# Column-wise Newton rounds, lookups by halving additions, and a new pace for the gathered expert rows in a two-layer diffusion backbone

## The chip, the cores and the metric

The kernel runs on one core of a Trainium2 chip. The metric is the device time of one execution in microseconds (us); a kernel's time is the median of its runs. Engines are named as the profile names them: PE (TensorE matmul), PEld (its weight loads), DVE (VectorE), ACT (ScalarE), POOL (GpSimd), SP (SyncE, whose queue issues most DMAs).

## The reference

Two layers over 256 latent tokens and 256 context tokens of width 1024, all in float32. The part that matters here is what surrounds the norms and the expert layer:

```python
def _rmsnorm(x, g):
    y = xf * lax.rsqrt(jnp.mean(xf * xf, axis=-1, keepdims=True) + EPS)
    return (y * g).astype(x.dtype)

# per layer: h = modulate(rmsnorm(x)); three token mixers; x += gate * mix
#            h2 = modulate(rmsnorm(x)); x += gate * _peer(h2)

def _peer(h, w_pq, peer_keys, peer_down, peer_up):        # 8 heads, 128 x 128 = 16384 experts
    s = einsum("blhpd,hpkd->blhpk", q, peer_keys)
    sv, si = lax.top_k(s, 16)                             # two sets of 16 per head
    cand = sv[..., 0, :, None] + sv[..., 1, None, :]
    cidx = si[..., 0, :, None] * 128 + si[..., 1, None, :]
    top_s, pos = lax.top_k(cand, 16)
    eidx = take_along_axis(cidx, pos)                     # the lookup
    gate = softmax(top_s)
    a = einsum("tkd,td->tk", peer_down[eidx], h)
    return einsum("tk,tkd->td", gate * gelu(a), peer_up[eidx])
```

## The kernel before

Activations lie transposed, 128 of the 1024 features in the partitions and tokens in the free dimension. Every weight is loaded by SP in pieces of 128x512 (`wpart`, L75 to L83), split by ACT into a high part (`wh`, L81) and by DVE into the remainder (`wl`, L82), and used in three matmuls (`mm3`, L91 to L93, or L789 to L791 for the up projection). So each matmul group waits for an SP load, an ACT copy and a DVE subtraction, and anything that stands ahead of that subtraction on DVE, which works in order, holds up PE.

**Norms.** `rstd` sums squares with matmuls against ones (L221), forms the mean (L225), and `newton` (L232 to L238) takes the inverse square root: a first guess (L234) and three rounds of three DVE instructions, each on the result of the one before. Its 128x2 operands hold one column for each block of 128 tokens. Then two scaled identities (L229), a broadcast by matmul (L245), four multiplications (L271), the modulation (L283) and the split (L285, L286) follow, and only then can the next matmuls (L91) start.

**Routing.** `topk` finds 16 of 112 candidates per head and then looks up the two key indices of each: a one-hot tile of 4 heads x 16 x 16 in bf16 is made (L607), multiplied with the indices (L612) and summed over one axis (L614), once for each of two index sets and two groups of four heads. It runs six times (24 sums in all): two times for the context tokens of layer 0, woven into the attention, and four times in `routes`.

**Experts of layer 0.** 128 of the context tokens take their 128 experts each by gathering (`rows`): 256 units, each an indirect DMA of 128 rows of 4 KB issued by POOL (L693) into one of three `gx` buffers, and one DVE pass over 128x1024: a dot product with `hot` for a down row (L706), or a weighted accumulation for an up row (L713). A gather is issued two units ahead, so its buffer comes free when the unit before the current one has been worked. The other 384 tokens go densely through all 128 blocks of 128 experts (`experts`, a step for each block): 18 matmuls of 512 columns, and for blocks from 60 on also the down projection with 24 matmuls of 384 columns. For the first 60 blocks that projection was done earlier and its result lies in DRAM (`E0`); SP loads it (`ge<-E`, L743), and DVE multiplies it with the gates (L752) and splits it (L754, L755). Steps are worked four blocks ahead.

`experts_both` calls the generator of units at a pace: `ROWS_S` units a step while the block ahead is still one of the 60, `ROWS_N` afterwards. Here "the first part" is the steps with loaded blocks and "the second part" those with a down projection. What is left of the units is drained after the last step (`drain(rows)`, L913), before the norm of layer 1. The instruction order of each engine comes from a scheduler that works from this program order.

Of the kernel before, what the change touches and what calls it, by code (L numbers as in the profile page):

```python
# [16 lines left out]
OP = mybir.AluOpType  # L17
AX = mybir.AxisListType
# [8 lines left out]
WINDOWS = (2, 4, 8, 16)  # L27
TG = 16
EARLY0, EARLY1 = 60, 88
ROWS_O, ROWS_A, ROWS_S, ROWS_N = 1, 0.5, 0.4, 2.6  # L30
SC0, SC1, R0, R1 = 0.5, 0.5, (0.36, 0.46, 0.34), (0.53, 0.9, 0.66)
FILL = (0, 3, 6)
PARTS = ((1, 3), (2, 5), (4,))
# [6 lines left out]
class Net:  # L40
# [191 lines left out]
    def newton(self, v, r, t):  # L232
        nc = self.nc
        nc.vector.tensor_scalar(r.bitcast(I32), v.bitcast(I32), -0.5, float(0x5F3759DF), op0=OP.mult, op1=OP.add)  # L234
        for _ in range(3):
            nc.vector.scalar_tensor_tensor(t, r, -0.5, r, op0=OP.mult, op1=OP.mult)
            nc.vector.tensor_mul(t, t, v)
            nc.vector.scalar_tensor_tensor(r, t, 1.5, r, op0=OP.add, op1=OP.mult)  # L238

    def bcast(self, dg):  # L240

# [319 lines left out]
    def topk(self, sv, si, out):  # L561
        nc, kp = self.nc, self.k
        ts = kp.tile([128, 8, 16], F32, name="tsc", bufs=1)
        pos = kp.tile([128, 128], U32, name="pos", bufs=1)


        for h4 in range(2):
            cd = self.f2([128, 4, 112])
            ra, rb = sv[:, 8 * h4:8 * h4 + 8:2, :], sv[:, 8 * h4 + 1:8 * h4 + 8:2, :]
            nc.vector.tensor_tensor(cd[:, :, 0:64].rearrange("p h (a b) -> p h a b", a=4),  # L570
                                    ra[:, :, 0:4].unsqueeze(3).to_broadcast([128, 4, 4, 16]),
                                    rb.unsqueeze(2).to_broadcast([128, 4, 4, 16]), op=OP.add)
            nc.vector.tensor_tensor(cd[:, :, 64:112].rearrange("p h (a b) -> p h a b", a=12),
                                    ra[:, :, 4:16].unsqueeze(3).to_broadcast([128, 4, 12, 4]),
                                    rb[:, :, 0:4].unsqueeze(2).to_broadcast([128, 4, 12, 4]), op=OP.add)
            for i in range(4):
                hd = 4 * h4 + i
                scr = self.f1([128, 112])
                yield from self.top16(ts[:, hd, :], pos[:, hd * 16:(hd + 1) * 16], cd[:, i, :], scr)
                yield  # L580

        sb = kp.tile([128, 2, 128, 2], BF, name="sb", bufs=1)
        for d in range(2):
            nc.vector.tensor_copy(sb.rearrange("p w (h a) d -> p w h a d", h=8)[:, :, :, :, d],
                                  si.rearrange("p (h w) a -> p w h a", w=2))
        g = kp.tile([128, 8, 16], F32, name="gate", bufs=1)
        sm = kp.tile([128, 8, 2], F32, name="gsum", bufs=1)
        nc.vector.tensor_sub(g, ts, ts[:, :, 0:1].to_broadcast([128, 8, 16]))
        nc.scalar.activation(g, g, AF.Exp)
        nc.vector.reduce_sum(sm[:, :, 0], g, axis=AX.X)  # L590
        nc.vector.reciprocal(sm[:, :, 1], sm[:, :, 0])
        nc.vector.tensor_mul(g, g, sm[:, :, 1:2].to_broadcast([128, 8, 16]))
        pu = self.f2([128, 4, 128], U32)
        nc.vector.tensor_scalar(pu[:, 0, :], pos, 4, None, op0=OP.logical_shift_right)
        nc.vector.tensor_scalar(pu[:, 1, :], pos, 2, None, op0=OP.logical_shift_right)
        nc.vector.tensor_scalar(pu[:, 2, :], pos, 15, None, op0=OP.bitwise_and)
        nc.vector.tensor_scalar(pu[:, 3, :], pos, 3, None, op0=OP.bitwise_and)
        pb = kp.tile([128, 2, 128], BF, name="pb", bufs=1)
        nc.vector.scalar_tensor_tensor(pb[:, 0, :], pu[:, 1, :], -12.0, pu[:, 0, :], op0=OP.add, op1=OP.max)
        nc.vector.scalar_tensor_tensor(pb[:, 1, :], pu[:, 0, :], 4.0, pu[:, 2, :], op0=OP.is_lt, op1=OP.mult)  # L600
        nc.vector.tensor_tensor(pb[:, 1, :], pb[:, 1, :], pu[:, 3, :], op=OP.max)
        ij = kp.tile([128, 2, 128], F32, name="ij", bufs=1)
        for w in range(2):
            for h4 in range(2):
                ks = slice(64 * h4, 64 * h4 + 64)
                oh = self.f2([128, 4, 16, 16], BF)
                nc.vector.tensor_tensor(  # L607
                    oh, self.iota16.unsqueeze(1).to_broadcast([128, 4, 16, 16]),
                    pb[:, w, ks].rearrange("p (h k) -> p h k", h=4).unsqueeze(2).to_broadcast([128, 4, 16, 16]),
                    op=OP.is_equal)  # L610
                o4 = oh.rearrange("p h a (k d) -> p (h a) k d", d=2)
                nc.vector.tensor_tensor(o4, o4, sb[:, w, ks, :].unsqueeze(2).to_broadcast([128, 64, 8, 2]), op=OP.mult)  # L612
                yield
                nc.vector.reduce_sum(ij[:, w, ks].rearrange("p (h k) -> p h k", h=4),  # L614
                                     oh.rearrange("p h a k -> p h k a"), axis=AX.X)
                yield
        out += [ij, g]

# [490 lines left out]
```

## Time and profile before

| | |
|---|---|
| median of 3 runs | 3106.73 us (3104.7 to 3107.01) |
| the profiled execution's own time | 3093.76 us |
| its span | 3092.0 us |
| PE, PEld busy | 2896.5 us (94%), 2597.3 us (84%) |
| DVE busy | 2341.6 us (76%) |
| ACT, POOL busy | 1443.6 us (47%), 322.3 us (10%) |
| DMA | 708.36 MB, mean 229 GB/s |

The span runs from the first to the last instruction of the profiled execution. That execution took 13 us less than the median of the runs shown; durations are read from it, and the median is what a prediction has to meet. PE is the busiest engine, but its share is a mean over stages, and matmuls overlap, so a busy PE is not one at its peak.

### The profile page before, as it was taken

To read this page: it belongs to the slowest core of one execution; us is meant where nothing else is said; L and a number is where in the kernel's file an instruction comes from. 1 tells how busy PE (TensorE), PEld (TensorE's weight loads), DVE (VectorE), ACT (ScalarE), POOL (GpSimd) and SP (SyncE) were. 2 spreads that over 40 slices of the span, in tenths; PEclk is the share of its full clock that TensorE was granted. 3 is DMA by queue.
4 is the path that set the end of the run, shared out by engine and by line. 5 is a ranking of instruction groups with operands and counts; after the bars stand their busy time and mean duration, and the time that the engine had idled before them with its cause. 6 is when DMAs were issued, how large, how long until landed. Compare 5 with 4: busy or idle time off the path is not lost.

```text
span 3092.0 us, 53067 instructions
## 1 busy us (share of the span) xinstructions
PE 2896.5 (94%) x18335; PEld 2597.3 (84%) x18335; DVE 2341.6 (76%) x5278; ACT 1443.6 (47%) x2820; POOL 322.3 (10%) x260
## 2 busy tenths in 40 slices
PE   7999899798999999999999996699999999999998
PEld 5799878798999777799998995589889998788997
DVE  6677779889988566688787887755799886676666
ACT  5565444443444333344433332354545555555554
POOL 0000000121000011134333344000000000000000
PEclk8999999999999999999999997799999999999999
DMA  7574443676666877799898987543657778888664
GB/s 249 171 233 144 139 129 116 213 249 199 199 221 213 289 251 263 248 309 327 314 320 308 319 294 264 177 152 123 186 159 228 242 235 283 296 267 286 203 201 141
DMA packets 413519, 708.36 MB, mean 229 GB/s; under 512 B 38336, under 2 KB 160960, under 8 KB 409152
## 3 DMA queue, kind: packets, MB, share of 16 engines
q1 hardware_dynamic: 376384, 570.73, 56.4%
q0 software_dynamic: 36864, 134.23, 13.2%
q8 instruction: 143, 2.34, 0.3%
q14 instruction: 128, 1.05, 0.1%
HBM read 638.49 MB, written 66.32 MB: 228 GB/s over the span
## 4 chain that ended last, share of the span: by engine, by line
PE 43%; DMA 10%; DVE 7%; issue 3%; POOL 1%; ACT 1%; DVEq 0%; SPq 0%; ACTq 0%; POOLq 0%
PE acc L790 6%; PE mm L91 6%; PE acc L791 6%; PE mm L92 6%; PE acc L789 6%; PE mm L93 6%; DMA gx<-in_up,eidx 3%; DMA ge<-E 3%; DVE wl L82 2%; DMA raw<-in_up 1%; DMA gx<-in_down,eidx 1%; PE acc L662 1%; PE acc L91 1%; PE acc L92 1%; PE acc L93 1%
## 5 line engine op out<-in xcount | busy, mean ns | idle before, releaser
L81 ACT CAST wh<-raw 128x512 fp32r<-128x512 f32 x1604 | 973.7, 618 | 834.1 <-PE mm L93 196.3
L82 DVE TENSOR_TENSOR wl<-raw,wh 128x512 fp32r<-128x512 f32 x1604 | 1079.8, 689 | 278.7 <-ACT wh L81 269.3
L91 PE MATMUL mm<-hH,wh 128*128 128x256 f32 (+1 forms) x2432 | 755.6, 311 | 12.8 <-ACT ge L731 8.0
L92 PE MATMUL mm<-hH,wl 128*128 128x256 f32 (+1 forms) x2432 | 748.9, 308 | 12.5 <-DVE wl L82 12.5
L93 PE MATMUL mm<-hL,wh 128*128 128x256 f32 (+1 forms) x2432 | 746.2, 307 | 0.0
L790 PE MATMUL acc<-wl,f 128*128 128x512 f32 x1280 | 506.6, 396 | 16.8 <-DVE wl L82 15.7
L789 PE MATMUL acc<-wh,f 128*128 128x512 f32 x1280 | 502.9, 393 | 5.0 <-ACT f L754 5.0
L791 PE MATMUL acc<-wh,f 128*128 128x512 f32 x1280 | 502.3, 392 | 0.0
L92 PEld LDWEIGHTS mm<-hH,wl 128*128 128x128 f32 x2432 | 467.2, 192 | 19.5 <-DVE wl L82 15.0
L91 PEld LDWEIGHTS mm<-hH,wh 128*128 128x128 f32 x2432 | 466.8, 192 | 18.9 <-ACT ge L731 9.1
L93 PEld LDWEIGHTS mm<-hL,wh 128*128 128x128 f32 x2432 | 466.2, 192 | 0.1
L790 PEld LDWEIGHTS acc<-wl,f 128*128 128x128 f32 x1280 | 242.1, 189 | 77.4 <-DVE wl L82 30.4
L693 POOL DMA_INDIRECT gx<-in_down,eidx x128 | 169.7, 1326 | 1295.5 <-DVE f L713 566.0
L789 PEld LDWEIGHTS acc<-wh,f 128*128 128x128 f32 x1280 | 242.3, 189 | 53.4 <-ACT f L754 5.3
L791 PEld LDWEIGHTS acc<-wh,f 128*128 128x128 f32 x1280 | 242.0, 189 | 49.9
L752 DVE TENSOR_TENSOR ge<-ge,f 128x256 f32<-128x256 f32 (+1 forms) x384 | 136.5, 380 | 180.5 <-DMA ge<-E 147.9
L754 ACT CAST f<-ge 128x384 fp32r<-128x384 f32 (+1 forms) x256 | 117.1, 459 | 284.3 <-DVE ge L752 278.2
L731 ACT ACTIVATE ge<-mm 128x384 f32<-128x384 f32 (+1 forms) x256 | 112.0, 438 | 222.2 <-PE mm L93 215.3
L91 PE MATMUL acc<-hH,wh 128*128 128x256 f32 x688 | 210.2, 306 | 2.0 <-ACT hH L285 2.0
L713 DVE SCALAR_TENSOR_TENSOR f<-gx,av,f 128x1024 f32<-128x1024 f32 x128 | 164.0, 1282 | 56.8 <-DMA gx<-in_up,eidx 56.4
L706 DVE CUSTOM_DVE_ANT_0 gx<-gx,f 128x1024 f32<-128x1024 f32 x128 | 156.3, 1221 | 60.4 <-DMA gx<-in_down,eidx 60.2
L92 PE MATMUL acc<-hH,wl 128*128 128x256 f32 x688 | 199.2, 290 | 0.9 <-DVE wl L82 0.9
(221 smaller groups left out, 3840.8 us busy)
## 6 DMA issues: line engine op xcount, KB each, us to landing
raw<-in_downT SPq DMA_DIRECT2D x512, 256.0 KB, 4.0
raw<-in_up SPq DMA_DIRECT2D x512, 256.0 KB, 4.3
raw<-in_wmod SPq DMA_DIRECT2D x192, 256.0 KB, 3.8
raw<-in_winc SPq DMA_DIRECT2D x172, 256.0 KB, 3.1
G<-f SPq DMA_DIRECT2D x40, 1024.0 KB, 6.0
f<-G SPq DMA_DIRECT2D x32, 1024.0 KB, 7.2
raw<-in_wpq SPq DMA_DIRECT2D x96, 256.0 KB, 3.4
raw<-in_wo SPq DMA_DIRECT2D x48, 256.0 KB, 2.6
```

The costliest lines, as they stand in the source:

```text
L81: nc.scalar.copy(H, r)
L82: self.last = nc.vector.tensor_sub(L, r, H.bitcast(F32)).ins
L91: t.matmul(out, lhsT=wH, rhs=xH, start=first, stop=False)
L92: t.matmul(out, lhsT=wL, rhs=xH, start=False, stop=False)
L93: t.matmul(out, lhsT=wH, rhs=xL, start=False, stop=last)
L693: nc.gpsimd.indirect_dma_start(out=r, out_offset=None, in_=self.h["up"][0] if up else self.h["down0"], in_offset=bass.IndirectOffsetOnAxis ...
L706: nc.vector.tensor_tensor_reduce(r, r, hot[:, 0, :], op0=OP.mult, op1=OP.add, scale=1.0, scalar=0.0, accum_out=av[:, k:k + 1])
L713: nc.vector.scalar_tensor_tensor(hot[:, 1, :], r, av[:, k:k + 1], hot[:, 1, :], op0=OP.mult, op1=OP.add)
L752: nc.vector.tensor_mul(y, y, Gg[:, :, c, :])
L789: m(p[t][half], lhsT=aH[:, a], rhs=H[:, 0], start=(i == 0), stop=False)
L790: m(p[t][half], lhsT=aH[:, a], rhs=L[:, 0], start=False, stop=False)
L791: m(p[t][half], lhsT=aL[:, a], rhs=H[:, 0], start=False, stop=(i == 127))
```

## The change

Three things change: `newton` works each column by itself with two dependent instructions a round (the factor of -0.5 is put into `v` once); the sum of each lookup becomes three additions of halves in place and a fourth that writes the result; and the pace of the gathered units becomes 0.75 and 2.75 a step, from 0.4 and 2.6.

```diff
-ROWS_O, ROWS_A, ROWS_S, ROWS_N = 1, 0.5, 0.4, 2.6
+ROWS_O, ROWS_A, ROWS_S, ROWS_N = 1, 0.5, 0.75, 2.75
...
     def newton(self, v, r, t):
         nc = self.nc
         nc.vector.tensor_scalar(r.bitcast(I32), v.bitcast(I32), -0.5, float(0x5F3759DF), op0=OP.mult, op1=OP.add)
+        nc.vector.tensor_scalar(v, v, -0.5, None, op0=OP.mult)
+
+        cs = [slice(i, i + 1) for i in range(v.shape[1])]
         for _ in range(3):
-            nc.vector.scalar_tensor_tensor(t, r, -0.5, r, op0=OP.mult, op1=OP.mult)
-            nc.vector.tensor_mul(t, t, v)
-            nc.vector.scalar_tensor_tensor(r, t, 1.5, r, op0=OP.add, op1=OP.mult)
+            for c in cs:
+                nc.vector.scalar_tensor_tensor(t[:, c], r[:, c], r[:, c], v[:, c], op0=OP.mult, op1=OP.mult)
+            for c in cs:
+                nc.vector.scalar_tensor_tensor(r[:, c], t[:, c], 1.5, r[:, c], op0=OP.add, op1=OP.mult)
...
-                nc.vector.reduce_sum(ij[:, w, ks].rearrange("p (h k) -> p h k", h=4),
-                                     oh.rearrange("p h a k -> p h k a"), axis=AX.X)
+
+                for n in (8, 4, 2):
+                    nc.vector.tensor_tensor(oh[:, :, 0:n], oh[:, :, 0:n], oh[:, :, n:2 * n], op=OP.add)
+                nc.vector.tensor_tensor(ij[:, w, ks].rearrange("p (h k) -> p h k", h=4), oh[:, :, 0], oh[:, :, 1],
+                                        op=OP.add)
```

In the changed kernel lines after `newton` stand 4 further on, and those after the lookup 7. The first place is DVE at the end of the layer-0 expert steps and into the norm that follows, in the kernel before. L820 (24 instructions) adds the experts' result to `xT`, L225 opens the norm, L706 and L713 are the two kinds of gathered unit.

```order
2605 L706 ISA gx,av<-gx,f_3782 128x1024
2606 L706 ISA av 128x1
2607 L175 MEMSET f_21222 128x512
2608 L820 SCALAR_TENSOR_TENSOR xT<-acc,mods_93,xT 128x128 x24
2609 L713 SCALAR_TENSOR_TENSOR f_3782<-gx,av,f_3782 128x1024
2610 L706 ISA gx,av<-gx,f_3782 128x1024
2611 L706 ISA av 128x1
2612 L713 SCALAR_TENSOR_TENSOR f_3782<-gx,av,f_3782 128x1024
```

The same place in the changed kernel, from the last gathered unit (L720 is what L713 was, L827 what L820 was, L762 what L755 was).

```order
2670 L720 SCALAR_TENSOR_TENSOR f_3810<-gx,av,f_3810 128x1024
2671 L759 TENSOR_TENSOR ge<-ge,f_20464 128x256
2672 L759 TENSOR_TENSOR ge<-ge,f_20466 128x128
2673 L82 TENSOR_TENSOR wl<-raw,wh 128x512
2674 L762 TENSOR_TENSOR f_21096<-ge,f_21095 128x384
2675 L82 TENSOR_TENSOR wl<-raw,wh 128x512 x6
2676 L175 MEMSET f_21302 128x512
2677 L827 SCALAR_TENSOR_TENSOR xT<-acc,mods_93,xT 128x128 x24
2678 L176 CAST f_21302<-sc_87 128x16x4
```

No gathered unit stands behind the `xT` updates any more: before, 235 of the 256 stood ahead of the first of them and 21 behind, now all 256 stand ahead. Counted by the splits of the blocks on DVE (L755), the fourth block's split had 23 units ahead of it and the 56th 43; now it is 24 and 62.

The second place is the norm ahead of layer 1's routing on DVE, before. L82 is a weight's subtraction, L236 to L238 one Newton round; two rounds of three are shown.

```order
2983 L236 SCALAR_TENSOR_TENSOR rs<-rs 128x2
2984 L82 TENSOR_TENSOR wl<-raw,wh 128x512
2985 L237 TENSOR_TENSOR rs<-rs 128x2
2986 L82 TENSOR_TENSOR wl<-raw,wh 128x512
2987 L238 SCALAR_TENSOR_TENSOR rs<-rs 128x2
2988 L236 SCALAR_TENSOR_TENSOR rs<-rs 128x2
2989 L237 TENSOR_TENSOR rs<-rs 128x2
2990 L82 TENSOR_TENSOR wl<-raw,wh 128x512
2991 L238 SCALAR_TENSOR_TENSOR rs<-rs 128x2
```

The same two rounds in the changed kernel (L240 is the first step of a round, L242 the second, each once for a column).

```order
3018 L240 SCALAR_TENSOR_TENSOR rs<-rs 128x1 x2
3019 L242 SCALAR_TENSOR_TENSOR rs<-rs 128x1
3020 L82 TENSOR_TENSOR wl<-raw,wh 128x512
3021 L242 SCALAR_TENSOR_TENSOR rs<-rs 128x1
3022 L240 SCALAR_TENSOR_TENSOR rs<-rs 128x1 x2
3023 L242 SCALAR_TENSOR_TENSOR rs<-rs 128x1
3024 L82 TENSOR_TENSOR wl<-raw,wh 128x512
```

Between L225 and L229 of this norm 9 subtractions stood before, and 6 stand now. On PE, ACT and SP few instructions moved (165 of 19617 on PE), and POOL's order is the same.

## Rows read from the trace of the kernel before

**Rows 1.** Windows: stretch, its length, busy us (and instructions) of PE, PEld, DVE, ACT, POOL, then PEclk, DMA share, GB/s.

```profile
1040.00:1283.00 243.00, 227.84 (x954) 179.58 (x953) 151.01 (x309) 92.99 (x173) 25.60 (x20) 0.98 0.76 258
1318.00:1854.00 536.00, 533.87 (x2694) 484.25 (x2693) 431.16 (x724) 210.79 (x406) 201.93 (x164) 1.00 0.91 313
1886.00:1957.00 71.00, 26.73 (x91) 18.75 (x90) 51.87 (x100) 16.57 (x34) 27.59 (x23) 0.57 0.69 235
```

**Rows 2.** The last two of these windows, for instructions on the tile gx alone.

```profile
1318.00:1854.00 536.00, 0.00 (x0) 0.00 (x0) 202.41 (x164) 0.00 (x0) 201.93 (x164) 1.00 0.91 313
1886.00:1957.00 71.00, 0.00 (x0) 0.00 (x0) 30.72 (x25) 0.00 (x0) 27.59 (x23) 0.57 0.69 235
```

**Rows 3.** Timeline of PE: last expert matmul, first of layer 1 (start, length, idle before).

```profile
1885.72 0.39 PE L791 MATMUL acc<-wh,f 128*128 128x512 f32 x1
...
1957.19 0.58 PE L91 MATMUL acc<-hH,wh 128*128 128x256 f32 x1 [0.76 <-ACT hH L285]
```

**Rows 4.** Timeline of DVE in the same stretch.

```profile
1895.07 6.17 DVE L820 SCALAR_TENSOR_TENSOR xT<-acc,mods,xT 128x128 f32<-128x128 f32 x24
...
1907.54 1.22 DVE L706 CUSTOM_DVE_ANT_0 gx<-gx,f 128x1024 f32<-128x1024 f32 x1 [1.56 <-DMA gx<-in_down,eidx]
...
1936.27 1.28 DVE L713 SCALAR_TENSOR_TENSOR f<-gx,av,f 128x1024 f32<-128x1024 f32 x1 [1.77 <-DMA gx<-in_up,eidx]
...
1954.56 1.28 DVE L271 TENSOR_TENSOR f<-xT,mm 128x512 f32<-128x512 f32 x2
```

**Rows 5.** Timeline of PE, then of DVE, at the later norm of layer 1.

```profile
2199.32 1.62 PE L221 MATMUL mm<-ones,f 128*128 128x1 f32 x14
...
2215.72 0.24 DVE L206 TENSOR_TENSOR mods<-mm,bmod 128x8 f32<-128x8 f32 x2 [1.84 <-PE mm L202]
...
2216.77 2.48 DVE L271 TENSOR_TENSOR f<-xT,mm 128x512 f32<-128x512 f32 x4
```

**Rows 6.** Timelines of SP, POOL and DVE in the first part.

```profile
1246.88 0.33 SPq L743 DMA_DIRECT2D ge<-E  x1
1252.32 0.33 SPq L743 DMA_DIRECT2D ge<-E  x1
...
1246.06 0.94 POOL L693 DMA_INDIRECT gx<-in_down,eidx  x1 [12.86 <-DVE f L713]
...
1251.19 0.63 DVE L752 TENSOR_TENSOR ge<-ge,f 128x256 f32<-128x256 f32 x2 [3.14 <-DMA ge<-E]
1254.76 0.63 DVE L752 TENSOR_TENSOR ge<-ge,f 128x256 f32<-128x256 f32 x2 [1.26 <-DMA ge<-E]
```

**Rows 7.** Waits of DVE, 1300 to 1850 us: total us, times, longest us.

```profile
DVE gx L706 <- DMA gx<-in_down,eidx: 48.1, 33, 4.3
```

**Rows 8.** Groups of DVE instructions by line: count, busy us, mean ns of one, idle before.

```profile
L656 DVE TENSOR_TENSOR a<-f,gT 128x1536 bf16<-128x1536 bf16 x160 | 148.7, 961 | 5.8 <-PE acc L662 5.8
...
L614 DVE TENSOR_REDUCE ij<-f 128x64 f32<-128x1024 bf16 x24 | 50.7, 2111 | 0.0
...
L607 DVE TENSOR_TENSOR f<-iota16b,pb 128x1024 bf16<-128x1024 bf16 x24 | 16.4, 698 | 0.0
```

**Rows 9.** Windows in which lookups run: one of layer 0, one of layer 1.

```profile
800.00:850.00 50.00, 49.55 (x393) 47.35 (x392) 47.47 (x99) 23.00 (x43) 0.00 (x0) 1.00 0.61 190
...
2300.00:2350.00 50.00, 40.44 (x322) 39.18 (x321) 50.00 (x163) 21.79 (x41) 0.00 (x0) 0.93 0.52 164
```

**Rows 10.** Timeline of DVE in two norms: one chain of Newton steps, then two side by side.

```profile
1972.16 0.16 DVE L236 SCALAR_TENSOR_TENSOR rs<-rs 128x2 f32<-128x2 f32 x1
1972.35 0.16 DVE L237 TENSOR_TENSOR rs<-rs 128x2 f32<-128x2 f32 x1
...
1980.82 0.15 DVE L237 TENSOR_TENSOR rs<-rs 128x2 f32<-128x2 f32 x1
1980.89 0.15 DVE L236 SCALAR_TENSOR_TENSOR rs<-rs 128x2 f32<-128x2 f32 x1
1981.01 0.16 DVE L238 SCALAR_TENSOR_TENSOR rs<-rs 128x2 f32<-128x2 f32 x1
```

## Prediction before the run

> **What bounds the kernel now.** I read the windows first, to find where PE does not work. In the second part of the layer-0 expert steps PE is the bound: 533.87 of 536 us busy at a granted clock of 1.00, 2694 matmuls [rows 1]. In the first part it is busy for 227.84 of 243 us with PEld at 179.58, so something holds it up a little. In the 71 us behind the last step it works for 26.73 us, and the clock falls to 0.57. That is the one long hole of the program, and DVE is busy there for 51.87 us.
>
> Next I asked what fills the hole. The same windows for the tile gx show 25 gathered units in it, 30.72 us of DVE [rows 2]. The last expert matmul ends at 1886.1 us, the first matmul of layer 1 starts at 1957.19 [rows 3], and 21 of the units stand on DVE between the `xT` updates and that matmul, with the steps of the norm between them. They come no faster than their gathers land: from 1907.54 to 1936.27 eleven units start, 2.87 us apart, and DVE waits for the transfer ahead of both ends [rows 4]. So the hole is as long as the units that were left over, and PE waits for the norm that is strung between them. The pace of the units decides how many are left.
>
> **The pace: the hole.** In the order of the changed program no unit is left behind the `xT` updates, so the norm runs alone. How long is that? The later norm of layer 1 is the same code without units: from its first sum of squares at 2199.32 to the end of its four multiplications at 2219.25 (2216.77 + 2.48) it takes 19.9 us [rows 5]. I add 1.4 us from the last multiplication to the first matmul, as in the hole (1954.56 + 1.28 to 1957.19) [rows 3, 4]. Ahead of it stand the transposes and the 24 updates, 6.17 us in one row [rows 4], which then start some 1 us behind the last matmul instead of 9 (1895.07), and 1 us to the first sum: 1886.1 + 1 + 6.2 + 1 + 21.3 = 1915.6. PE is slow after a pause (clock 0.57 in the hole) [rows 1]: 14 sums of squares took 1.62 us in the later norm [rows 5], so 32 take 3.7, and at 0.57 of that speed 6.5, or +2.8. Three weight subtractions fewer stand in the Newton chain (6 for 9, about 0.6 us each: -1.8), and the later norm's wait of 1.84 us for its modulation sums [rows 5] does not apply here. That gives 1914.8, 29 us behind the last matmul: the hole shrinks by 42 us. Bounds: 36 us if the modulation matmuls that share the stretch come late, 48 us if the norm takes no longer than the shortest reading.
>
> **The pace: the first part.** Between the splits of block 4 and block 56 now stand 38 units instead of 20, so 18 more gathers and 18 more DVE passes. DVE has room (151.01 of 243 us busy). What it waits for there is the load of `E`: with a gather just issued (1246.06) the load issued at 1246.88 lets DVE go on at 1251.19, 4.31 us later; the next one, without a gather, takes 2.44 us (1252.32 to 1254.76) [rows 6]. The wait comes in most steps, and the next load is issued only when the split behind it is done, so a later load is a later step. Lower bound: 0, if the passes fall into waits and the slower loads are hidden by PE's backlog. Upper bound: each gather costs its whole transfer, 128 x 4 KB = 0.524 MB at the 313 GB/s of the busiest stretch [rows 1], 1.68 us, or 30 us; the pair of loads gives 1.87 us, about the same. Many waits already have a gather beside them, and these are not made longer twice; I take the middle, +15 us.
>
> **The pace: the second part.** Between block 56 and block 128 stand 194 units instead of 184. The step is now 536 us / (2694 / 42.7) = 8.5 us (42 matmuls and two thirds of one for the modulation), for 2.6 units. DVE has 431.16 of 536 us, and ten passes of 1.25 us lie in its gaps. The cover is PE's own work. It is not complete: DVE already waits 33 times for a down row in 550 us, up to 4.3 us [rows 7]. I take +2 us, bounds 0 and 10 x 1.68 = 17.
>
> **The lookups.** One sum takes 2.11 us [rows 8]. The four additions have 512, 256, 128 and 64 results. In bf16 1024 results take 698 ns and 1536 take 961 [rows 8], 0.51 ns a result and 170 ns for the instruction; that gives 435, 303, 238 and about 200 ns, 1.18 us together, 0.93 us less. There are 24, so DVE gains 22 us; the path gains less. In the window of layer 1's routing DVE works for 50.00 of 50 us and PE for 40.44, while in that of layer 0 PE has 49.55 [rows 9]. Four sums in the window of layer 1 count whole (3.7), its other four half (1.9), and the sixteen of layer 0 for 1.4 together: -7 us. Bounds: -2 and -15.
>
> **Newton.** Before: nine steps in a chain, 0.19 us from start to start (1972.16 to 1972.35), although one takes 0.16. Where two independent chains run side by side, the other chain's step starts 0.07 us behind, and the first goes on 0.19 us after its own start (1980.82, 1980.89, 1981.01) [rows 10]. So two columns side by side cost the time of one: six links of 0.2 us instead of nine, -0.55 us a norm, and the factor for `v` falls beside the first guess. The scheduler also sets fewer weight subtractions into the chain: 12 fewer over the norms outside the hole, 0.6 us each. Only six other norms have PE waiting behind them, and a subtraction that is moved back is needed there too, so of 0.55 x 6 + 12 x 0.6 = 10.5 us I take -3. Bounds: -8 and +4 (four more instructions of 0.16 us in six norms, if nothing overlaps). The final norm's one column wins under 1 us, counted in this.
>
> A rule speaks against this. The Trainium skill, VectorE: DVE Perf Modes (Terms), says that every DVE instruction is followed by a flush, and that the next can't issue until the pipe is empty; its section "Side-by-side: where the cycles go for N=2048 bf16" gives about 150 cycles at 0.96 GHz for the start alone. By that an independent neighbour hides nothing, and the sum would end at +4 for Newton instead of -3. The trace shows starts 0.07 us apart, so here I go by the rows.
>
> **Sum.** -42 + 15 + 2 - 7 - 3 = -35 us. Against the profiled execution's own 3093.8 us (span 3092.0) that is 3059. The runs shown have a median 13 us above that execution, and I take the difference over: 3106.7 - 35 = **3072 us**.
>
> **Rivals.**
> 1. *The new transfers cost all they can.* First part +30, second part +17, the rest as above: -42 + 47 - 10 = -5, or 3102 us, no change. For it: DMA is busy for 0.76 and 0.91 of the two parts, and the load next to a gather came 1.9 us late. Against it: PE's records in the second part are without gaps. With only the first part in full it is -20, or 3087 us. Chance of the former 0.04, of the latter 0.14.
> 2. *The transfers are free and the lookups count in full.* First part +3, lookups -12: -52, or 3055 us. For it: E waits of one step leave PE with work in most steps. Chance 0.17.
> 3. *The ring of gathers becomes the bound of the second part* (the other side). Three buffers turn around in one issue, one landing and one pass. 2.75 units in 8.5 us need one every 3.09 us; the hole shows 2.87 us with PE quiet. If the loaded ring can do no better than 3.5 us, a step takes 9.6 us, and 71 steps lose 80 us: 3106.7 - 35 - 2 + 80 = 3150 us. It decides from 3.28 us a unit on, where 71 steps lose the 37 us that all else gains. For it: the pace now is 536 / 164 = 3.27 us a unit [rows 2], and DVE waits for gathers there. Against it: PE never waits there, so 3.27 is PE's pace and not the ring's. Chance 0.05.
> 4. *Two columns do not overlap*: a 128x1 step that hangs on the one before it does not start under its neighbour, four more instructions of 0.16 us stand in six norms, Newton costs +4, and the time is 3079 us, inside the range of the forecast. For it: all of a norm's steps are short and of one kind. Against it: the interleaved chains [rows 10]. Chance 0.1. This is what the Trainium skill's page VectorE: DVE Perf Modes (Terms) would have.
>
> **How the numbers follow.** The forecast itself has 0.5 (its own range 3059 to 3085), the rivals the rest. Rival 4 is faster too, and so are rival 2 and the milder rival 1: 0.5 + 0.1 + 0.17 + 0.14 = 0.91 for faster by over 0.2% (6 us, which is about what a measurement of this kernel can tell from no change). Same has 0.04, slower 0.05. The range takes in rival 2 and the milder rival 1 with the errors of their terms: 3046 to 3094; what is left out is the full rival 1, rival 3 and the tails of the forecast, below 2 in 10.
>
> **What would show it.** In the profile after: no unit on DVE behind the `xT` updates, and the first matmul of layer 1 some 29 us behind the last expert matmul instead of 71. The first part, now 4.75 us a step (243 us for 954 / 18.7 steps), longer by about 0.3 us a step, with longer waits for `E`. The second part at 8.5 us a step still, and PE without gaps. The four additions at about 1.2 us together. Newton links 0.2 us apart with both columns inside one. The prediction is wrong if the second part's step grows beyond 9 us, if the first part grows by more than 30 us, or if the norm behind the experts still takes over 50 us with no unit in it.

## The result and the profile after

| | before | changed |
|---|---|---|
| median of 4 runs each, same chip | 3105.72 us (3092.85 to 3107.01) | 3059.24 us (3056.73 to 3060.92) |
| ratio, 95% interval | | 0.9865 [0.9834, 0.9895] |
| profiled execution, span | 3093.76 us, 3092.0 us | 3060.92 us, 3059.2 us |

The changed kernel is faster by 42 us by the ratio (0.0135 of 3105.72), with an interval of 33 to 52; the two medians lie 46.5 us apart. The prediction was 3072 us with a range of 3046 to 3094. Of the two profiled executions that of before was one of its shorter ones, so the traces differ by 32.8 us only. What is read from them is split by place first.

**The hole.** The windows of the changed kernel, in the columns of [rows 1]; the third is its hole, from the last expert matmul to the first matmul of layer 1.

```profile
1040.00:1283.00 243.00, 225.48 (x934) 179.57 (x932) 167.37 (x329) 91.53 (x169) 54.74 (x37) 0.96 0.83 288
1318.00:1854.00 536.00, 524.00 (x2611) 469.34 (x2610) 426.79 (x714) 199.37 (x394) 198.87 (x168) 1.00 0.90 312
1901.00:1929.00 28.00, 20.96 (x92) 17.95 (x90) 18.83 (x63) 13.49 (x28) 0.00 (x0) 0.70 0.30 98
```

The timeline of PE there, which answers to [rows 3] (L798 is what L791 was).

```profile
1900.87 0.40 PE L798 MATMUL acc<-wh,f 128*128 128x512 f32 x1
...
1929.10 0.63 PE L91 MATMUL acc<-hH,wh 128*128 128x256 f32 x3 [0.97 <-ACT hH L289]
```

The timeline of DVE there, which answers to [rows 4].

```profile
1901.74 6.29 DVE L827 SCALAR_TENSOR_TENSOR xT<-acc,mods,xT 128x128 f32<-128x128 f32 x24 [2.64 <-PE acc L824]
...
1917.34 0.16 DVE L225 TENSOR_SCALAR rs<-mm 128x2 f32<-128x2 f32 x1 [7.43 <-PE mm L221]
...
1919.38 0.34 DVE L240 SCALAR_TENSOR_TENSOR rs<-rs 128x1 f32<-128x1 f32 x2
1919.64 0.15 DVE L242 SCALAR_TENSOR_TENSOR rs<-rs 128x1 f32<-128x1 f32 x1
1919.73 0.69 DVE L82 TENSOR_TENSOR wl<-raw,wh 128x512 fp32r<-128x512 f32 x1
1920.34 0.15 DVE L242 SCALAR_TENSOR_TENSOR rs<-rs 128x1 f32<-128x1 f32 x1
1920.41 0.34 DVE L240 SCALAR_TENSOR_TENSOR rs<-rs 128x1 f32<-128x1 f32 x2
...
1925.20 2.48 DVE L275 TENSOR_TENSOR f<-xT,mm 128x512 f32<-128x512 f32 x4 [0.53 <-PE mm L249]
```

No unit stands there any more, and POOL issues nothing in the third window. From 1901.27 (1900.87 + 0.40) to 1929.10 the hole is 27.8 us long; before it was 71.1 (1886.11 to 1957.19). That is 43.3 us less. The runs further down bear the size out: in all with no unit left behind the steps the hole takes 26.6 to 30.3 us. In the two others with 21 units left the first matmul of layer 1 came after 65.2 and 53.7 us, so 71.1 is one trace's number. But the way from the last expert matmul to the end of the program took 1205.9 us in the kernel before and 1162.4 with the new pace alone, 43.5 less.

**The expert steps** cost some of it. The last expert matmul ends 15.2 us later than before, although at 1000 us DVE's instructions came 3.5 us earlier (each paired with the same one of before), so the steps lost 18.7 us. In the first part PE issued 934 matmuls in 243 us: a step of 4.87 us (243 / (934 / 18.7)), against 4.76, or 5 us over 52 steps. In the second part there are 2611 matmuls for 2694 in 536 us, a step of 8.76 us for 8.49: 17 us over the 63 steps of the window (13 by what is left of the 18.7). The same windows for the tile gx answer to [rows 2].

```profile
1040.00:1283.00 243.00, 0.00 (x0) 0.00 (x0) 46.10 (x37) 0.00 (x0) 54.74 (x37) 0.96 0.83 288
1318.00:1854.00 536.00, 0.00 (x0) 0.00 (x0) 206.26 (x169) 0.00 (x0) 198.87 (x168) 1.00 0.90 312
```

In the second part 169 units are worked, one each 3.17 us. A pace of 2.75 a step wants one each 3.07 us if the step is to take 8.44 us, PE's own pace in the runs further down. The waits of DVE for gathers in this stretch (in total, times, longest, us), first in the kernel before:

```profile
DVE gx L706 <- DMA gx<-in_down,eidx: 47.5, 32, 4.3
DVE f L713 <- DMA gx<-in_up,eidx: 40.6, 27, 3.7
```

and in the changed kernel, with one of PE's own waits behind them:

```profile
DVE gx L713 <- DMA gx<-in_down,eidx: 54.1, 31, 4.0
DVE f L720 <- DMA gx<-in_up,eidx: 43.9, 28, 4.6
```

```profile
PE acc L797 <- DVE wl L82: 7.0, 10, 2.5
```

PE now waits for weight subtractions, which stand on DVE behind a unit that waits for its gather. One such place in the timeline of DVE:

```profile
1398.01 1.22 DVE L713 CUSTOM_DVE_ANT_0 gx<-gx,f 128x1024 f32<-128x1024 f32 x1
...
1401.69 1.28 DVE L720 SCALAR_TENSOR_TENSOR f<-gx,av,f 128x1024 f32<-128x1024 f32 x1 [2.46 <-DMA gx<-in_up,eidx]
1405.65 1.23 DVE L713 CUSTOM_DVE_ANT_0 gx<-gx,f 128x1024 f32<-128x1024 f32 x1 [2.67 <-DMA gx<-in_down,eidx]
```

and in that of POOL:

```profile
1395.62 1.43 POOL L700 DMA_INDIRECT gx<-in_down,eidx  x1 [0.30 <-DVE ge L759]
1399.50 0.94 POOL L700 DMA_INDIRECT gx<-in_up,eidx  x1 [2.45 <-DVE av L713]
1403.25 0.94 POOL L700 DMA_INDIRECT gx<-in_down,eidx  x1 [2.81 <-DVE f L720]
1407.15 0.94 POOL L700 DMA_INDIRECT gx<-in_up,eidx  x1 [2.97 <-DVE av L713]
```

Read it as a ring: the pass at 1398.01 frees a buffer, and POOL, which waited for that (releaser L713), issues the next gather at 1399.50. The down row issued at 1395.62 is worked at 1405.65, ten microseconds later, and its buffer is issued anew at 1407.15. Three buffers that come round in 11.5 us give one unit in 3.8 us here.

**The rest** of the 32.8 us, 8.2 us, is what is left for lookups and Newton in these two executions: 3.5 ahead of the expert steps, the others behind them. The groups of the four additions, which answer to L614 in [rows 8]:

```profile
L620 DVE TENSOR_TENSOR f<-f 128x512 bf16<-128x512 bf16 x24 | 10.0, 417 | 0.0
L620 DVE TENSOR_TENSOR f<-f 128x256 bf16<-128x256 bf16 x24 | 6.8, 283 | 0.0
L620 DVE TENSOR_TENSOR f<-f 128x128 bf16<-128x128 bf16 x24 | 5.2, 217 | 0.0
L621 DVE TENSOR_TENSOR ij<-f 128x64 f32<-128x64 bf16 x24 | 5.2, 216 | 0.1
```

Together 1.13 us, against 2.11 for the one sum.

### The profile page after: what moved, and what is told of

It reads as the page before. It is cut to its first block, busy times and chain, and to the rows that moved or that the text cites. A ratio compares the mean times of both kernels' runs of the same rounds, so it can differ in the third digit from the quotient of the medians.

```text
span 3059.2 us, 53181 instructions
## 1 busy us (share of the span) xinstructions
PE 2898.7 (95%) x18335; PEld 2600.2 (85%) x18335; DVE 2314.6 (76%) x5402; ACT 1436.2 (47%) x2820; POOL 323.0 (11%) x260
## 3 DMA queue, kind: packets, MB, share of 16 engines
q14 instruction: 128, 1.05, 0.1%
## 4 chain that ended last, share of the span: by engine, by line
PE 59%; DMA 16%; DVE 16%; issue 6%; ACT 2%; POOL 1%; DVEq 0%; SPq 0%; ACTq 0%; POOLq 0%
PE mm L91 7%; PE mm L92 7%; PE mm L93 7%; PE acc L797 5%; PE acc L798 5%; PE acc L796 5%; DMA gx<-in_up,eidx 4%; DVE wl L82 4%; DMA ge<-E 4%; PE acc L92 3%; PE acc L93 3%; PE acc L91 3%; DMA gx<-in_down,eidx 3%; PE acc L669 2%; DVE a L663 1%
## 5 line engine op out<-in xcount | busy, mean ns | idle before, releaser
L82 DVE TENSOR_TENSOR wl<-raw,wh 128x512 fp32r<-128x512 f32 x1604 | 1074.4, 685 | 276.4 <-ACT wh L81 267.2
L798 PE MATMUL acc<-wh,f 128*128 128x512 f32 x1280 | 503.5, 394 | 0.0
L798 PEld LDWEIGHTS acc<-wh,f 128*128 128x128 f32 x1280 | 243.3, 190 | 49.7
L713 DVE CUSTOM_DVE_ANT_0 gx<-gx,f 128x1024 f32<-128x1024 f32 x128 | 155.9, 1218 | 65.3 <-DMA gx<-in_down,eidx 63.5
L720 DVE SCALAR_TENSOR_TENSOR f<-gx,av,f 128x1024 f32<-128x1024 f32 x128 | 163.6, 1278 | 52.0 <-DMA gx<-in_up,eidx 51.9
```

What stands on the lines that cost most here:

```text
L82: self.last = nc.vector.tensor_sub(L, r, H.bitcast(F32)).ins
L713: nc.vector.tensor_tensor_reduce(r, r, hot[:, 0, :], op0=OP.mult, op1=OP.add, scale=1.0, scalar=0.0, accum_out=av[:, k:k + 1])
L720: nc.vector.scalar_tensor_tensor(hot[:, 1, :], r, av[:, k:k + 1], hot[:, 1, :], op0=OP.mult, op1=OP.add)
L798: m(p[t][half], lhsT=aL[:, a], rhs=H[:, 0], start=False, stop=(i == 127))
```

## The experiments

Each ratio is to the kernel before, run on the same chip (medians 3098.41, 3097.19 and 3097.95 us in the three groups: first four, next four, last three).

**One part of the change alone.** The first three take the kernel before and make one part of the change: the pace, `newton`, the lookups.

```diff
# e1
-ROWS_O, ROWS_A, ROWS_S, ROWS_N = 1, 0.5, 0.4, 2.6
+ROWS_O, ROWS_A, ROWS_S, ROWS_N = 1, 0.5, 0.75, 2.75
# e2: newton with two dependent instructions a round and column
+        nc.vector.tensor_scalar(v, v, -0.5, None, op0=OP.mult)
...
# e3
-                nc.vector.reduce_sum(ij[:, w, ks].rearrange("p (h k) -> p h k", h=4),
...
+                for n in (8, 4, 2):
+                    nc.vector.tensor_tensor(oh[:, :, 0:n], oh[:, :, 0:n], oh[:, :, n:2 * n], op=OP.add)
...
```

> The kernel before with only the new pace of the gathered units (0.75 and 2.75). Theory from the two traces: the hole behind the expert steps shrinks by 43 us and the expert steps grow by 17 to 20 us, most of it in the second part, so -23 to -26 us against the kernel before. Rival, the pace is all there is: -33 us or more, as the whole change. Rival, the pace is worth less alone because the norm in the hole also gained from the new Newton rounds: about -20 us.

> The kernel before with only the column-wise Newton rounds. Forecast of the prediction: -3 us (bounds -8 and +4). Theory now: the chain is shorter by 0.5 us a norm where PE waits, and fewer weight subtractions stand in it, so -2 to -4 us. Rival, no overlap of the two columns: +1 to +4 us.

> The kernel before with only the lookups by additions of halves. Forecast of the prediction: -7 us (bounds -2 and -15), nearly all of it in layer 1's routing, where DVE is the bound. Rival, PE's backlog covers the lookups everywhere: 0 to -2 us.

The pace alone: 3074.88 us, ratio 0.9932 [0.9913, 0.9951], so -21 us (-15 to -27). Newton alone: 3096.25 us, 0.9996 [0.9985, 1.0007], no change that can be measured. The lookups alone: 3077.63 us, 0.9943 [0.9925, 0.9962], -18 us (-12 to -23). The three add up to -40, and the whole gave -42: they work side by side. By this ratio the lookups give 2.5 times what was predicted. Where? Each DVE instruction was paired with the same one of the kernel before. In this run those of 520 us come 7 us early and those of 600 us 14 us, but 4 of these were there before the first lookup. After layer 1's routing the lead has grown by 8 again. Two windows of the kernel before in the stretch of the first eight sums (462 to 557 us), and then one window of the run with the lookups alone:

```profile
440.00:480.00 40.00, 38.07 (x281) 34.32 (x279) 35.01 (x84) 17.05 (x36) 0.00 (x0) 1.00 0.31 97
520.00:560.00 40.00, 37.63 (x283) 34.28 (x283) 37.79 (x84) 19.20 (x41) 0.00 (x0) 1.00 0.36 112
```

```profile
520.00:560.00 40.00, 38.51 (x303) 36.50 (x302) 36.45 (x100) 18.66 (x39) 3.96 (x4) 1.00 0.45 138
```

PE is not full there: DVE is busy for 37.79 of 40 us and PE falls behind by 2 us in 40. With the additions PE issues 303 matmuls in the same window for 283 (the run is also 7 us ahead there). The window at 800 us, which the prediction read for layer 0 [rows 9], says nothing of these eight.

The lead of a single trace can't size this term: at 440 us, ahead of any lookup, it lies between 6 us late and 4 early. Its growth can, and the traces of all ten runs with the additions agree on it: 6.8 to 6.9 us from 440 to 565 us, across the first eight sums, and 7.6 to 9.4 from 2250 to 2500, across layer 1's eight. In the two runs without the additions (pace alone, Newton alone) it grows by 0.0 us in the first stretch and shrinks by 0.3 to 0.4 in the second. Together that is some 15 us, inside the interval of the ratio.

**Other paces.** Four numbers for the pace of the changed kernel, all else kept.

```diff
-ROWS_O, ROWS_A, ROWS_S, ROWS_N = 1, 0.5, 0.75, 2.75
+ROWS_O, ROWS_A, ROWS_S, ROWS_N = 1, 0.5, 1.1, 2.4     # e4
+ROWS_O, ROWS_A, ROWS_S, ROWS_N = 1, 0.5, 0.4, 3.0     # e6
+ROWS_O, ROWS_A, ROWS_S, ROWS_N = 1, 0.5, 1.8, 1.85    # e7
+ROWS_O, ROWS_A, ROWS_S, ROWS_N = 1, 0.5, 0.9, 2.55    # e9
```

> The changed kernel with 1.1 units a step in the first part and 2.4 in the second (all units are still done ahead of the last step). Theory: the units are cheap in the first part (about 0.3 us each) and dear in the second, where the ring of three gather buffers is near its limit and DVE waits for gathers in front of weight subtractions; so the second part falls back to 8.5 us a step or less (-15 to -20 us), the first grows by 6 to 10 us, and the time is 5 to 12 us below the changed kernel. Rival, each gather costs its transfer wherever it stands: no change (within 3 us). Rival, the first part is at its limit of loads at 0.75: it grows by 20 us or more and the time is above the changed kernel.

> The changed kernel with 0.4 units a step in the first part, as before, and 3.0 in the second. Ring theory: the ring gives a unit each 3.1 to 3.2 us, so a step of the second part takes 9.3 to 9.6 us; 71 steps cost 45 to 60 us more than the changed kernel's 8.76, less 5 us in the first part, and the time is 30 to 55 us above the changed kernel, near or above the kernel before. Rival, a unit costs the same wherever it stands: no change within 5 us.

> The changed kernel with 1.8 units a step in the first part and 1.85 in the second. The first part's step of 4.8 us holds no more than 1.5 units of 3.1 us, so by the ring theory it grows to 5.6 us or more (+45 us for 56 steps against the changed kernel's first part), the second part is PE's alone (8.3 to 8.4 us a step, -25 us), and the time is 15 to 25 us above the changed kernel. Rival, the first part stays cheap at 0.35 us a unit: +20 and -25, about the changed kernel or below.

> The changed kernel with a pace of 0.9 and 2.55 units a step, between the changed kernel's 0.75 and 2.75 and the 1.1 and 2.4 of the run that was fastest so far (ratio 0.9807). Theory (a ring of three buffers turns one unit around in about 3.1 us, so a step of 8.43 us has room for some 2.7 units, and a unit in the first part costs 0.24 us up to 0.4 to 0.75 and 0.45 us up to 1.1 a step): the second part runs at PE's own pace (PE busy for 536 of 536 us, 2700 matmuls or more), the first part is some 4 us shorter than at 1.1 and 2.4, no unit is left behind the last step, ratio 0.979 to 0.980. Rival (the second part is lost to the units' bytes or passes, a little with each unit): the second part lies between the two, some 2660 matmuls in 536 us, and the ratio is 0.983 or above.

With 1.1 and 2.4: 3038.07 us, 0.9807 [0.9785, 0.9829]. With 0.4 and 3.0: 3085.22 us, 0.9957 [0.994, 0.9974]. With 1.8 and 1.85: 3076.3 us, 0.993 [0.991, 0.9949]. With 0.9 and 2.55: 3037.32 us, 0.9799 [0.9778, 0.9819]. The windows of the two parts, first for 1.1 and 2.4:

```profile
1040.00:1283.00 243.00, 216.36 (x889) 171.77 (x888) 180.18 (x338) 85.32 (x161) 74.36 (x53) 0.95 0.89 315
1318.00:1854.00 536.00, 536.00 (x2711) 487.57 (x2710) 423.01 (x709) 221.08 (x409) 199.83 (x153) 1.00 0.88 303
```

for 0.4 and 3.0 (the second part, and then PE's longest sum of waits in it):

```profile
1318.00:1854.00 536.00, 504.21 (x2461) 443.88 (x2460) 419.89 (x698) 186.34 (x374) 204.49 (x174) 0.99 0.90 310
```

```profile
PE acc L797 <- DVE wl L82: 25.1, 27, 2.5
```

for 1.8 and 1.85 (the first part; it lasts to 1330 us there, so the second window isn't all second part):

```profile
1040.00:1283.00 243.00, 205.02 (x812) 154.94 (x811) 200.43 (x357) 80.78 (x148) 92.76 (x78) 0.96 0.97 348
```

and for 0.9 and 2.55:

```profile
1040.00:1283.00 243.00, 220.78 (x908) 174.67 (x907) 171.76 (x331) 86.82 (x164) 61.63 (x44) 0.96 0.87 299
1318.00:1854.00 536.00, 535.23 (x2699) 485.13 (x2698) 430.54 (x721) 211.40 (x408) 198.52 (x162) 1.00 0.91 313
```

In the second part the step is 8.44 us at 2.4 units, 8.47 at 2.55, 8.76 at 2.75, 9.29 at 3.0. It breaks off where the units would have to come closer than some 3.1 us: asked for 3.0 a step the kernel still brings only one each 3.1 us (174 in 536), and PE waits. In the first part the step is 4.87 us at 0.75, 5.00 at 0.9, 5.11 at 1.1 and 5.60 at 1.8, where the DMA engines are busy for 0.97 of the time. So a unit more in each step costs 0.3 us up to 0.75 ((4.87 - 4.76) / 0.35) and 0.7 us from there to 1.8 ((5.60 - 4.87) / 1.05). The intervals of 0.9 and 2.55 and of 1.1 and 2.4 lie over each other; both beat the changed kernel, by 18 and 20 us (0.9865 - 0.9807 and 0.9865 - 0.9799 of 3098). The former is more than the 5 to 12 us expected. With 0.4 and 3.0 the time is 28 us above the changed kernel, a little under the expected 30 to 55; with 1.8 and 1.85 it is 20 above, as expected.

**A ring of four buffers.** The changed kernel with four `gx` buffers and gathers issued three ahead; to make room, two other pools are smaller.

```diff
-name="gx", tag="gx", bufs=3)
+name="gx", tag="gx", bufs=4)
-                ahead.append(gather(*units[n + 2]))
+                ahead.append(gather(*units[n + 3]))
-name="f1", tag="f1", bufs=6)
+name="f1", tag="f1", bufs=4)
-name="f2", tag="f2", bufs=14)
+name="f2", tag="f2", bufs=13)
```

> The changed kernel with four gather buffers and three units gathered ahead (to make room, two work buffers of 1 KB and one of 2 KB are taken away). Ring theory: the second part at 2.75 units a step is slow because the three buffers turn round too slowly; with four it goes back to 8.5 us a step, PE without gaps (about 2690 matmuls in the 536 us from 1318 us, for 2611 now), and the time falls by 10 to 20 us. Rival, the bytes of the gathers take the bandwidth: the second part stays at 8.7 us or more a step. Rival, the taken buffers cost elsewhere: the second part is quicker and the time is not.

3052.94 us, ratio 0.9855 [0.9838, 0.9871]: as the changed kernel. But the second part is another one. Its window, and the waits of DVE for gathers in it:

```profile
1318.00:1854.00 536.00, 536.00 (x2712) 487.76 (x2711) 448.11 (x744) 224.81 (x411) 240.11 (x175) 1.00 0.92 325
```

```profile
DVE gx L713 <- DMA gx<-in_down,eidx: 9.7, 11, 2.1
DVE f L720 <- DMA gx<-in_up,eidx: 3.2, 6, 0.9
```

At the same pace of 2.75 more units are worked (176) and more bytes moved (325 GB/s for 312), with more DVE work, and yet DVE waits 12.9 us for gathers for 98.0, and PE not at all. DVE's order is also the same there: 805 of 806 instructions between the splits of blocks 60 and 128 stand in the changed kernel's order. So neither the bytes nor the passes slowed the second part but the turn of three buffers. The 20 us that this gives (101 matmuls more, 0.2 us each) are mostly lost elsewhere: against before, PE is 2 to 10 us late in the first part of this run (1080 to 1260 us), where in the changed kernel it is between 4 us early and 4 late, and of a lead of 54 us at 2680 it keeps 40. The smaller pools are the other edit, and the scheduler set DVE's first part in another order too (of 281 instructions that are not units 224 keep theirs); which of them costs what was not tried.

**Units taken apart.** The first of these is the changed kernel without any gather and pass (it leaves out the experts of 128 context tokens of layer 0); the other two work at 1.1 and 2.4, one with the passes but without the gathers (each pass works on a resident tile), the other with the gathers but with passes of 32 of 1024 columns.

```diff
# e8 and e10: no gather
-            nc.gpsimd.indirect_dma_start(out=r, out_offset=None, in_=self.h["up"][0] if up else self.h["down0"],
-                                         in_offset=bass.IndirectOffsetOnAxis(ap=e[:, k:k + 1], axis=0))
# e8: no pass either
-                    nc.vector.tensor_tensor_reduce(r, r, hot[:, 0, :], op0=OP.mult, op1=OP.add, scale=1.0, scalar=0.0,
...
# e11: short passes
+                    nc.vector.tensor_tensor_reduce(r[:, 0:32], r[:, 0:32], hot[:, 0, 0:32], op0=OP.mult, op1=OP.add, scale=1.0, scalar=0.0,
```

> The changed kernel without any gathered unit (neither gather nor DVE pass; the experts of 128 context tokens of layer 0 are left out). It gives the floor. By the traces the first part loses its 8 to 10 us of growth and falls towards PE's 4.3 us a step (-25 us against the changed kernel's 4.86), the second part goes to 8.3 us a step (-30 us), and the earlier units in the attention of layer 0 give 10 us or less: 55 to 70 us below the changed kernel. If the hole still takes 28 us, all of it is the norm's own chain.

> The changed kernel at 1.1 and 2.4 units a step, without the gathers: each unit's DVE pass works on a tile that is resident (it leaves out the gathering of the experts' rows of 128 context tokens of layer 0). Without units at all the first part took 18 us less than in the kernel before, at 1.1 and 2.4 it took 13 us more: 31 us between them. Theory (the first part pays for the transfers: the load of E lands later when a gather moves beside it): most of the 31 us go, 1000 matmuls or more in 1040 to 1283 us against 889, and the whole comes to 2990 to 3005 us. Rival (it pays for DVE's time, 1.25 us a pass): few of them go, 890 to 930 matmuls, and 3025 to 3035 us.

> The changed kernel at 1.1 and 2.4 units a step, with all gathers, but each unit's DVE pass covers 32 of its 1024 columns (it leaves out the other 992 of each expert row of 128 context tokens of layer 0). Theory (the first part pays for the transfers): 885 to 920 matmuls in 1040 to 1283 us, as with whole passes, and a time of 3025 to 3038 us. Rival (it pays for DVE's time): 1000 matmuls or more there, and 2990 to 3005 us.

Without units 2988.15 us, 0.9653 [0.9637, 0.9669]. Passes alone 2988.48 us, 0.9649 [0.9621, 0.9678]. Transfers alone 3049.99 us, 0.9834 [0.9807, 0.9862]. The units cost the changed kernel 66 us in all (0.9865 - 0.9653 of 3098). Without gathers, 256 passes of 1.25 us (320 us of DVE) cost nothing in the total, though DVE's order is not the same in these two runs.

The cleanest pair is 1.1 and 2.4 with the gathers and without: DVE, PE and ACT have the same instructions in the same order in both, and the gathers cost 49 us (0.9807 - 0.9649 of 3098). Nearly all of it lies in the first part. From the split of block 4 to that of block 56 the run with gathers takes 252.3 us and the one without 210.6, or 0.8 us for each of 54 units; from block 60 to 128 they take 585.3 and 584.6. So in the second part the gathers are free as long as the ring keeps up. At 2.75 a step the same 68 blocks take 609.1 us, in the kernel before 590.6.

The first part with passes alone: its window (from some 1233 us on it holds steps with a down projection), DVE's wait for `E`, and the median time of the loads of `E` from issue to landing (the last figure of the row).

```profile
1040.00:1283.00 243.00, 243.00 (x1099) 204.44 (x1098) 210.72 (x390) 102.27 (x193) 0.00 (x0) 1.00 0.67 222
```

```profile
DVE ge L757 <- DMA ge<-E: 20.9, 16, 3.6
```

```profile
ge<-E SPq DMA_DIRECT2D x44, 192.0 KB, 3.2
```

PE is full. In the run without units the load took 3.5 us. In the kernel before, with 20 gathers in this stretch, the same load took 4.2 us and DVE waited for `E` 87.9 us in 36 waits:

```profile
DVE ge L752 <- DMA ge<-E: 87.9, 36, 4.7
```

```profile
ge<-E SPq DMA_DIRECT2D x50, 192.0 KB, 4.2
```

With transfers alone the first part got slower still than with whole passes, 823 matmuls where 885 to 920 had been expected. Its window and the wait for `E`:

```profile
1040.00:1283.00 243.00, 209.52 (x823) 160.40 (x822) 117.26 (x313) 80.23 (x151) 57.62 (x49) 0.93 0.85 294
```

```profile
DVE ge L759 <- DMA ge<-E: 110.7, 37, 9.7
```

The longest wait for `E` is 9.7 us there, 7.3 with whole passes. Why short passes make it worse isn't settled by these runs, because the length of the passes is not all that differs: the scheduler also set DVE's instructions in another order. Of the 278 that are not units between the splits of blocks 4 and 56, 242 keep their order; with passes alone all 278 do. So this run says nothing of what a pass costs beside a gather.

## Why the prediction was right, and where its sum was not

**The hole, -42.** Measured -43.3: the units were the hole, and 27.8 us was the length of the norm by itself, 28.7 in the prediction; without any unit in the program it took 27.0. Two of its parts cancelled: the 32 sums of squares took 8.5 us (1908.78 to 1917.3, with four other matmuls among them) instead of 6.5, at a granted clock of 0.70 in the window, but from the first of them to the end of the four multiplications it was 18.9 us (to 1927.68) where 20.9 had been added up.

**The first part, +15.** Mis-sized: +5. The mechanism holds, since the transfers are the price and the passes fall into waits (passes alone). But the step "longer waits for `E`" did not come. Against 87.9 us in 36 waits before, the changed kernel has:

```profile
DVE ge L759 <- DMA ge<-E: 74.4, 38, 4.7
```

The step grew by 0.1 us where 0.3 was foretold: eighteen gathers more cost 0.3 us each, where the middle of the bounds had 0.8 and the bytes 1.68. That the eighteen passes filled what had been waiting fits these rows, but no run shows it by itself. Nor did the load land much later with more gathers beside it: 4.3 us in the median with 38 of them (the run with four buffers), 4.2 with 20. The Trainium skill, DMA: Bandwidth & Descriptors (Queues, rings and completion order), says that each DMA engine takes turns between the queues that have work for it; by that a load of `E` beside a gather shares its engines, and the landing times of 3.2 and 3.5 us without gathers and 4.2 with them agree.

**The second part, +2.** This is the step that failed: "PE never waits there, so 3.27 is PE's pace and not the ring's". It was both, very nearly. The ring of three turns in 3.1 us a unit, PE's step of 8.44 us at 2.75 units wants 3.07, and the loss was 13 to 17 us, the upper bound of a term that had been worked out from bytes. The ring of four shows that it was not bytes. And at the new pace PE does wait, 7.0 us for weight subtractions. Rival 3 had named the mechanism and the wait; its price of 80 us hung on a ring of 3.5 us that nothing measured. The rows to hand were the 2.87 us between units in the hole [rows 4], where DMA was at 0.69 [rows 1], and the 88 us (47.5 and 40.6, in 59 waits) that DVE spent waiting for gathers in this part: a ring near its turn already. Expert steps together were foretold as +17 and came to +18.7, by two errors that cancelled.

The rule of thumb of the Trainium skill, DMA: Bandwidth & Descriptors (Anatomy of one DMA — SWDGE (gpsimd) path), 2.0 us and a microsecond for each 436 KB, gives an estimate of 3.2 us for one gather of 524 KB; with a pass of 1.25 us three buffers would then turn in 1.5 us a unit. The trace does not agree under this load: the gathers of the kernel before landed in 6.2 to 6.4 us in the median, and at the place shown of the changed kernel one took 10. No run here has a gather by itself.

**The lookups, -7.** Mis-sized: -18 alone by the ratio, with an interval of -12 to -23 that reaches inside the bound of -15, and some -15 by the growth of the lead. The price of the instructions was right (1.13 us for 1.18). Layer 1's share was 8.5 for 5.6. Layer 0's was taken as 1.4 for sixteen sums from a window in which PE was full; that is right for the eight sums near it (from 650 to 1000 us the lead does not grow in the run with the lookups alone, 13.8 and 13.9 us), but the first eight stand in a stretch where DVE is busy for 37.79 of 40 us, and gave 6.9.

**Newton, -3.** Measured -1, not to be told from nothing. The columns do overlap: L242 of the first column starts while L240 of the second runs (L240 twice in 0.34 us, L242 0.26 us behind the first start), and a subtraction starts 0.09 us after the start of an L242 that takes 0.15 us. The chain is shorter, so too little waited for it; that is what is left, and no run shows it by itself. Against rival 4 this is by the rows; the time alone would not tell them apart.

So the sum of -35 came out at -42 by the ratio: hole -43 and expert steps +19 (from the traces), lookups -18 and Newton -1 (from the ratios) give -43. Most of what was missing stood in the lookups, so part of the near hit is luck: the expert steps came right by two errors, and the price of the ring, which rival 3 had put at 80 us, stayed small because the 3.07 us a unit that was wanted is so close to the 3.1 that the ring gives. The forecast of 3072 us lay 13 us above the measured median; of the medians of before, the earlier was 1 us higher than the later.

## What to carry to other kernels

When a ring of buffers feeds an engine that works in order, work out its turn (issue, landing under the load of that stage, pass, divided by the buffers) before raising its pace: that PE does not wait at the present pace says only that the ring is not yet slower. Work that is moved to a part where an engine waits for transfers can be free in the engine and paid for in the transfers; price it by a run at another pace if there is one, since here a unit cost 0.3 to 0.8 us where its bytes had 1.68. An operation that runs in several stages needs a window for each, above all for those in which its own engine is nearly full. And where a scheduler sets the order, compare the order of each engine between two runs before a difference is put down to the edit.

## What the runs showed of the hardware

Without gathers beside them the DVE passes cost nothing in the total: 320 us of them, taken out or left in, gave 2988.15 and 2988.48 us. The gathers cost 0.8 us each beside the loads of `E` and next to nothing in the second part (585.3 and 584.6 us for the same 68 blocks), where the ring kept up. The gathers landed later at a higher rate (7.0 to 7.2 us in the median at 325 GB/s with four buffers, 6.2 to 6.4 before) without any loss to PE. With passes cut to a thirty-second, and another order of DVE's instructions, the stretch with loaded `E` was slower (823 matmuls for 889), for a reason that stays open.
